# Memory rows loaded behind the weights and kept unsplit, and matmul operands placed at chosen offsets modulo 256 bytes, in a one-core decoder-layer kernel

## The chip, the cores and the metric

The program runs on one core of one Trainium2 chip. The metric is the device time of one execution in microseconds, the median of several runs. A profiled execution gives the rows shown below; its own time stands beside the median. Engines are called by their names in the profile: PE (TensorE matmuls), PEld (TensorE weight loads), DVE (VectorE), ACT (ScalarE), POOL (GpSimd) and SP (SyncE, which here only issues DMAs).

## The reference

One layer of a hybrid decoder for two request groups with shared weights: 256 prompt rows and 8 rows of single-token decoding, together T = 264 rows of width 2048, all in float32.

```python
x = layer_norm(ALPHA * x + 0.5 * swiglu(x, ffn1_w1, ffn1_w3, ffn1_w2), ln1_g, ln1_b)     # FFN 1
mix, sh, cv, wkv = parallel_mixer(x, shift_prev, conv_prev, wkv_prev, p)                # RWKV-7 heads and convolution
x = layer_norm(ALPHA * x + mix, ln2_g, ln2_b)
x = layer_norm(ALPHA * x + mem_attend(x, mk, mv, w_mq, w_mo), ln3_g, ln3_b)             # 4 heads over 256 memory tokens
x = layer_norm(ALPHA * x + 0.5 * swiglu(x, ffn2_w1, ffn2_w3, ffn2_w2), ln4_g, ln4_b)    # FFN 2
mk, mv = mem @ w_mk, mem @ w_mv                                                         # prompt group, 256 memory rows
```

The FFNs are 2048 to 5632 and back. The outputs are the two groups' rows, the new states, and the memory keys and values `mk` and `mv`.

## The kernel before

Activations lie transposed: the 2048 features are 16 tiles of 128 partitions, each with 264 columns. Every float32 operand of a large product is split in two: a rounded high part (`hi`, made by an ACT copy to float32r) and the rest (`lo`, made by a DVE subtraction), at `split_from` (L153 to L155). A product is then three matmuls in `mm3` (L263 to L267): the activations are the moving operand, a 128 x 128 block of the weights is the stationary one, and the order is hi weights with hi activations, hi weights with lo activations, lo weights with hi activations. In `gemm` (L280) every feature tile k of the activations meets two such blocks, so one k is six matmuls in a row, all of them on the same two activation tiles (three where a weight tile is only 128 columns wide).

The weights stream from HBM. `fetch` (L214) issues 512 KB loads on SP into three `raw` tiles, `prepare` (L232) splits each into one of four `whi` and four `wlo` tiles of 128 x 1024, and `chunk` hands them to the matmuls, 24 matmuls for each. The order of the weight tiles is a plan made at the start (`plan_add`); raw loads run up to three tiles ahead of the splits, and the splits up to four ahead of the matmuls.

The stages follow the reference: FFN 1 (the trace's first 790 us), four units of the memory keys and values (`mem_kv`, L1292), the mixer, its output projection, the other units with the attention, its output projection, and FFN 2 (from about 1790 us). Side jobs (`Side`, `start`, `pump`) are Python generators that a planner steps between the matmuls. The framework then orders each engine's instructions; an instruction without a dependency on the matmuls may be issued much earlier than the place where the generator made it. `tc.issue_after(x)` puts the instructions of its block behind `x` where they are on the same engine's queue.

Operands of the large matmuls live here:
- `xh{k}`, `xl{k}`: the 16 split tiles of the layer's input (pool `act`), also the first 16 gate tiles of FFN 2
- `gh{i}`, `gl{i}`: the 22 gate tiles of half an FFN (pools `ffn1` and, for 16 to 21, `ffn2`)
- `rh{k}`, `rl{k}`: 16 split tiles of 266 columns (pool `raw`), the memory rows during the attention and then the rows that FFN 2 starts from; the normalised rows enter FFN 2 through them
- `mh{k}`, `ml{k}`: the split memory rows of 256 columns (pool `mem`)

A pool hands out its tiles one behind the other in the order in which their tags are first asked for, and pads a tile's row to a multiple of 32 bytes. The pools stand behind each other: `const`, `wraw`, `whi`, `wlo`, `act`, `tmp`, and then either `mem` with `ffn1` behind it, or `mix`, or `raw` with `att` or `ffn2` behind it. A row of 264 float32 is 1056 bytes, four times 256 and 32 more.

The memory rows are loaded in `mem_rows` (L1277, started at the 300th step of FFN 1) in four loads of 512 KB on SP (`split_in`, L169), split at once, and both parts are written to HBM by 32 DMAs on POOL (L1284). `mem_reload` (L1286) reads them back by 32 DMAs on POOL (L1290) once the mixer's pool is closed, during the mixer's output projection. Four tables (`lnv`, `mv`, `cw`, `sst`) are loaded by `loaded` (L138, DMA at L141) at the 100th step. `rst`, a constant of the recurrence with 520 columns, is a tile of `const` filled by two POOL memsets (L631, L632).

Of the kernel before, what the change touches and what calls it, by code (L numbers as in the profile page):

```python
# [8 lines left out]
F32 = mybir.dt.float32  # L9
F32R = mybir.dt.float32r  # L10
I32 = mybir.dt.int32
AF = mybir.ActivationFunctionType
ALU = mybir.AluOpType
# [5 lines left out]
KD = 16  # L19
TP = 256  # L20
TB = 8
T = TP + TB
DFF = 5632
# [4 lines left out]
C = 64  # L28
NC = TP // C
NP = 2 * NC  # L30
# [23 lines left out]
class Builder:  # L54
    def __init__(self, tc, I, O, es):
        self.tc, self.nc, self.I, self.O = tc, tc.nc, I, O
        P = lambda name, bufs, **kw: es.enter_context(tc.tile_pool(name=name, bufs=bufs, **kw))
        self.const = P("const", 1)
        self.wraw = P("wraw", NRAW)
        self.whi = P("whi", NSPLIT)  # L60
        self.wlo = P("wlo", NSPLIT)
        self.act = P("act", 1)
        self.tmp = P("tmp", 2)
        self.acc = P("acc", 4, space=PSUM)
        self.mis_stack = es.enter_context(ExitStack())
        self.banks()
        self.dram = P("dram", 1, space=DRAM)
        self.n = 0
        self.t = 0.0
        self.sides = []  # L70
        self.plan, self.raws, self.split = [], [], []
        self.nraw = self.nsplit = self.nused = self.nres = 0

    def banks(self, held=0):

        self.mis_stack.close()
        P = lambda name, bufs: self.mis_stack.enter_context(self.tc.tile_pool(name=name, bufs=bufs, space=PSUM))
        self.mis = P("mis", 4 - held)
        self.held = P("held", held) if held else None

    def uid(self, s):
        self.n += 1
# [55 lines left out]
    def loaded(self, name, shape):  # L138

        t = self.ct(shape, name)  # L140
        self.nc.sync.dma_start(t, self.I[name])  # L141
        return t

    def hold(self):

# [13 lines left out]
        lo = [self.act.tile([128, T], F32R, tag=f"xl{k}", name=self.uid("xl")) for k in range(KD)]  # L159
        return hi, lo  # L160

    def split_in(self, pool, src, n, hi, lo, between=None):

        W = 4

        def load(h):
            t = pool.tile([128, W, T], F32, tag="nat", name=self.uid("nat"), bufs=2)[:, :, :n]
            if between is None or h:
                self.nc.sync.dma_start(t, src[:, W * h : W * h + W])  # L169
            else:  # L170

                self.nc.sync.dma_start(t[:, :1], src[:, :1])
                between(1, (slice(0, 2),))
                self.nc.sync.dma_start(t[:, 1:], src[:, 1:W])
                between(1, (slice(2, 4),))
            return t

        loaded = [load(0)]
        if between is not None:
            between(EARLY)  # L180
        for h in range(KD // W):
            if h + 1 < KD // W:
                loaded.append(load(h + 1))
            yield LOAD
            for k in range(W):
                kk = W * h + k
                with self.hold():
                    self.first.append(self.split_from(loaded[h][:, k], hi[kk], lo[kk]))
                yield 1.5
# [24 lines left out]
    def fetch(self, ahead=NRAW, parts=(slice(None),)):  # L214
        nc = self.nc
        if parts[0].start == 2:
            src, kk, cc = self.plan[0]
            nc.sync.dma_start(
                self.raws[0].rearrange("p (k c) -> p k c", c=cc)[:, parts[0]],
                src.rearrange("(k p) c -> p k c", p=128)[:, parts[0]],  # L220
            )
            return
        while self.nraw < len(self.plan) and self.nraw < self.nsplit + ahead:
            src, kk, cc = self.plan[self.nraw]
            raw = self.wraw.tile([128, 1024], F32, tag="raw", name=self.uid("raw"))[:, : kk * cc]
            dst, src = raw.rearrange("p (k c) -> p k c", c=cc), src.rearrange("(k p) c -> p k c", p=128)
            for k in parts:
                nc.sync.dma_start(dst[:, k], src[:, k])
            self.raws.append(raw)
            self.nraw += 1  # L230

# [338 lines left out]
    def mixer_consts(self):  # L570
        nc, I, tc = self.nc, self.I, self.tc
# [14 lines left out]
        gp = nc.gpsimd  # L586
# [40 lines left out]
            for o in QS:  # L627
                gp.tensor_copy(self.lm[o, l], m[o, o])

        self.rst = self.ct([128, NP, C + 1], "rst")  # L630
        gp.memset(self.rst, 1.0)  # L631
        gp.memset(self.rst[:, :, 0:1], 0.0)  # L632

    def mcol(self, n, j, w=1):
        c = MV[n] + j
# [580 lines left out]
    def mixer(self, pool, P):  # L1216
        nc = self.nc
        self.mx = pool
        H = 30
        self.rows = {}  # L1220
        self.sa, self.vk = self.ct([128, 8, TB], "sa"), self.ct([128, 8, TB], "vk")
        self.last = self.mt("last", (128, 27, TB + 1))
        done = Side(self.tc, iter(()), 0)
        done.done = True
        self.convs, self.heads, self.decs, self.tails, self.cL = [done], [done], [done], {}, []
        self.S = [{} for _ in range(4)]
        for u in MIX_ORDER.split():
            kind, g = u[0], int(u[1])
            if kind == "l":
                yield from self.lora(P[u])  # L1230
            elif kind in "kvr":
                yield from self.rw_part(kind, g, P[u])
            else:
                yield from self.conv_part([2 * g, 2 * g + 1] if kind == "p" else [g], P[u])
# [42 lines left out]
    def mem_rows(self, pool):  # L1277
        self.mh = [pool.tile([128, TP], F32R, tag=f"mh{k}", name=self.uid("mh")) for k in range(KD)]
        self.ml = [pool.tile([128, TP], F32R, tag=f"ml{k}", name=self.uid("ml")) for k in range(KD)]
        yield from self.split_in(pool, self.I["mem"], TP, self.mh, self.ml)  # L1280
        self.mkeep = [self.dram.tile([2, 128, TP], F32R, tag=f"mem{k}", name=self.uid("mem")) for k in range(KD)]
        for k in range(KD):
            for i, t in enumerate((self.mh, self.ml)):
                self.nc.gpsimd.dma_start(self.mkeep[k][i], t[k])  # L1284

    def mem_reload(self):  # L1286
        self.mh, self.ml = self.rawtiles()
        for k in range(KD):
            for i, t in enumerate((self.mh, self.ml)):
                self.nc.gpsimd.dma_start(t[k][:, :TP], self.mkeep[k][i])  # L1290

    def mem_kv(self, unit, dest):  # L1292

# [358 lines left out]

PRETURN = 5
RAW, RENORM = 2, 0.6
TS = 384
LASTCOLS = [(1536, 256), (1792, 128), (1920, 128)]
CONV_GAP = 2.5
# [25 lines left out]
def program(tc, I, O):  # L1683
    with ExitStack() as es:
# [8 lines left out]
        P2 = b.ffn_plan(I["ffn2_w1"][0], I["ffn2_w3"][0], I["ffn2_w2"][0])  # L1693

        with tc.tile_pool(name="mem", bufs=1) as mpool:
            with tc.tile_pool(name="ffn1", bufs=1) as pool:
                b.xs = b.load_x(mpool)

                def ffn1():
# [29 lines left out]
        def after():  # L1729
            mix.close()  # L1730
            b.raw = es.enter_context(tc.tile_pool(name="raw", bufs=1))
            b.att_start(att.enter_context(tc.tile_pool(name="att", bufs=1)))

        b.drive(b.mixer_out(PX, after))
# [8 lines left out]
        att.close()  # L1743
        b.banks()
        with tc.tile_pool(name="ffn2", bufs=1) as pool:

            def ffn2():
                b.L = yield from b.ffn(pool, P2, b.L)
# [80 lines left out]
```

## Time and profile before

| what | us |
|---|---|
| median of 3 runs | 2542.96 (2537.16 to 2549.2) |
| the profiled execution's own time | 2542.35 |
| its span, first to last instruction | 2540.6 |

| engine | busy us | share of the span | instructions |
|---|---|---|---|
| PE | 2483.8 | 98% | 22328 |
| PEld | 2428.6 | 96% | 22328 |
| DVE | 1573.6 | 62% | 2529 |
| ACT | 1190.5 | 47% | 1786 |
| POOL | 282.1 | 11% | 466 |

Matmuls overlap, so one matmul's duration in the trace (some 0.28 us) is not what it costs; the distance from one start to the next is. A window of the trace names how many matmuls touch it, and the window's length over that count gives the distance. The two or so matmuls that straddle a window's edges are counted in it, so that 2.3 (0.28 us over 0.12 us) is taken off a window's count.

### The profile page before, as it was taken

What the parts mean: (1) busy time and instruction counts of PE and PEld (TensorE: products, weight loads), DVE (VectorE), ACT (ScalarE), POOL (GpSimd) and SP (SyncE); (2) the same over time, 40 slices, a digit from 0 to 9 for tenths busy, and PEclk for the clock granted to TensorE, in tenths of its full rate; (3) what the DMA queues carried; (4) which work ended last, traced back from release to release, by engine and by line L of the source; (5) the groups of instructions that cost most, each with busy time, mean ns of one, the idle gap of its engine ahead of it and who ended that gap; (6) DMA issues with size and microseconds to landing.
All of it is one profiled execution on the core that took longest, in us unless ns stands there. A gap on an engine that the chain in (4) does not pass through costs nothing. (4 is left out here: it accounts for less than half of the span.)

```text
span 2540.6 us, 53466 instructions
## 1 busy us (share of the span) xinstructions
PE 2483.8 (98%) x22328; PEld 2428.6 (96%) x22328; DVE 1573.6 (62%) x2529; ACT 1190.5 (47%) x1786; POOL 282.1 (11%) x466
## 2 busy tenths in 40 slices
PE   8999999999999999999989999999999999999998
PEld 8999999999999988988889889999999999999998
DVE  5644444444657598799767567779545445454564
ACT  5444333444445555455636355657444333444443
POOL 2400000000000001000130222220133400000000
PEclk9999999999999999999999999999999999999999
DMA  9655555555557754544386789975677755555553
GB/s 294 201 178 181 179 182 181 181 182 180 171 178 219 225 158 125 154 129 136 128 277 225 260 297 318 330 218 189 196 217 212 222 182 183 181 178 181 175 174 126
DMA packets 460083, 502.09 MB, mean 198 GB/s; under 512 B 22800, under 2 KB 427536, under 8 KB 459840
## 3 DMA queue, kind: packets, MB, share of 16 engines
q1 hardware_dynamic: 417840, 417.09, 52.3%
q0 software_dynamic: 28864, 71.42, 9.0%
q10 hardware_dynamic: 13136, 10.15, 1.2%
q8 instruction: 175, 2.87, 0.5%
q14 instruction: 68, 0.56, 0.1%
HBM read 479.86 MB, written 18.73 MB: 196 GB/s over the span
## 5 line engine op out<-in xcount | busy, mean ns | idle before, releaser
L155 DVE TENSOR_TENSOR wlo<-raw,whi 128x1024 fp32r<-128x1024 f32 (+1 forms) x791 | 959.1, 1213 | 865.7 <-ACT whi L154 861.4
L154 ACT ACTIVATE whi<-raw 128x1024 fp32r<-128x1024 f32 (+1 forms) x791 | 823.0, 1041 | 1052.1 <-PE acc L266 881.0
L265 PE MATMUL acc<-xh,whi 128*128 128x264 f32 x2864 | 832.2, 292 | 20.3 <-DVE y L1208 7.8
L266 PE MATMUL acc<-xl,whi 128*128 128x264 f32 x2864 | 821.9, 287 | 0.6 <-DVE xl L155 0.6
L267 PE MATMUL acc<-xh,wlo 128*128 128x264 f32 x2864 | 819.1, 287 | 1.2 <-issue 0.7
L265 PEld LDWEIGHTS acc<-xh,whi 128*128 128x128 f32 x2864 | 544.0, 190 | 29.6 <-issue 8.4
L266 PEld LDWEIGHTS acc<-xl,whi 128*128 128x128 f32 x2864 | 545.2, 190 | 3.9 <-DVE xl L155 1.0
L267 PEld LDWEIGHTS acc<-xh,wlo 128*128 128x128 f32 x2864 | 543.2, 190 | 3.3 <-DVE wlo L155 1.1
L265 PE MATMUL acc<-rh,whi 128*128 128x264 f32 (+2 forms) x1600 | 458.5, 287 | 0.2 <-ACT lnx L359 0.2
L267 PE MATMUL acc<-rh,wlo 128*128 128x264 f32 (+2 forms) x1600 | 455.9, 285 | 0.0
L266 PE MATMUL acc<-rl,whi 128*128 128x264 f32 (+2 forms) x1600 | 454.9, 284 | 0.0
L265 PE MATMUL acc<-gh,whi 128*128 128x264 f32 x1408 | 400.4, 284 | 1.7 <-ACT lnx L359 1.7
L267 PE MATMUL acc<-gh,wlo 128*128 128x264 f32 x1408 | 400.8, 285 | 0.0
L266 PE MATMUL acc<-gl,whi 128*128 128x264 f32 x1408 | 400.5, 284 | 0.0
L265 PEld LDWEIGHTS acc<-rh,whi 128*128 128x128 f32 x1600 | 302.1, 189 | 2.6 <-ACT lnx L359 0.5
L266 PEld LDWEIGHTS acc<-rl,whi 128*128 128x128 f32 x1600 | 301.2, 188 | 1.2
L267 PEld LDWEIGHTS acc<-rh,wlo 128*128 128x128 f32 x1600 | 301.5, 188 | 0.2
L265 PEld LDWEIGHTS acc<-gh,whi 128*128 128x128 f32 x1408 | 265.3, 188 | 2.0 <-ACT lnx L359 1.9
L267 PEld LDWEIGHTS acc<-gh,wlo 128*128 128x128 f32 x1408 | 264.9, 188 | 0.1
L266 PEld LDWEIGHTS acc<-gl,whi 128*128 128x128 f32 x1408 | 264.6, 188 | 0.0
L1141 DVE SCALAR_TENSOR_TENSOR y<-u,cw,y 128x256 f32<-128x256 f32 x240 | 111.7, 479 | 0.6
L1121 POOL MEMSET u<- 128x30 f32 x8 | 1.0, 131 | 787.9 <-DMA out<-mo 745.0
(350 smaller groups left out, 2132.0 us busy)
## 6 DMA issues: line engine op xcount, KB each, us to landing
raw<-in_ffn_w SPq DMA_DIRECT2D x509, 512.0 KB, 3.6
raw<-in_w_in SPq DMA_DIRECT2D x86, 512.0 KB, 3.6
raw<-in_w_mk SPq DMA_DIRECT2D x32, 512.0 KB, 3.3
raw<-in_w_mv SPq DMA_DIRECT2D x32, 512.0 KB, 5.4
raw<-in_w_out SPq DMA_DIRECT2D x32, 512.0 KB, 4.0
kv<-in_cache_mem_k POOLq DMA_DIRECT2D x32, 512.0 KB, 6.7
raw<-in_w_mq SPq DMA_DIRECT2D x32, 512.0 KB, 6.1
kv<-in_cache_mem_v POOLq DMA_DIRECT2D x32, 512.0 KB, 6.0
```

Source lines behind the costliest of these rows:

```text
L154: a = self.nc.scalar.activation(hi, src, AF.Copy)
L155: return a, self.nc.vector.tensor_tensor(lo, src, hi.bitcast(F32), ALU.subtract)
L265: nc.tensor.matmul(out, wh, xh, start=start, stop=False)
L266: nc.tensor.matmul(out, wh, xl, start=False, stop=False)
L267: self.mark = nc.tensor.matmul(out, wl, xh, start=False, stop=stop)
L1121: nc.gpsimd.memset(u[:, 0:H], 0.0)
L1141: V.scalar_tensor_tensor(c[:, :TP], u[:, i : i + TP], w(i), c[:, :TP], ALU.mult, ALU.add)
```

## The change

Four things change.

1. **Places.** Unused gap tiles and an order of first use fix where the moving operands begin modulo 256 bytes. `places` lays out pool `act`: a gap of 224 bytes, then for each two feature tiles `xh`, `xl`, `xh`, `xl`, followed by four `y` tiles or a gap of 128 bytes. `gate_places` does the like for the gate tiles with the gaps `GAPS[1]` and `GAPS[3]`; `rh` and `rl` stand in pairs with a gap of 128 bytes between pairs behind a first gap of `GAPS[2]`; pool `mem` begins with a gap of `GAPS[0]`.
2. **Held loads.** `behind` puts the loads of the four tables and of the memory rows behind the weight load that SP issued last where the generator made them.
3. **The kept memory rows.** The raw rows are written to HBM by four DMAs of 512 KB on POOL, straight from the loaded tiles. The reload is 16 DMAs of 128 KB on POOL into the `rl` tiles, and each is split again by an ACT copy and a DVE subtraction in place.
4. **`rst`** moves from pool `const` into pool `mix`, and its two memsets to the mixer's start.

```diff
     def __init__(self, tc, I, O, es):
...
         self.act = P("act", 1)
+        self.places()
         self.tmp = P("tmp", 2)
...
+    def place(self, pool, *tags):
+
+        for t in tags:
+            if isinstance(t, int):
+                if t:
+                    pool.tile([128, t // 4], F32, tag=self.uid("gap"), name=self.uid("gap"))
+            else:
+                tag, cols, dt = t
+                pool.tile([128, cols], dt, tag=tag, name=self.uid(tag))
+
+    def places(self):
+
+
+        order = [224]
+        for q in range(KD // 2):
+            for k in (2 * q, 2 * q + 1):
+                order += [(f"xh{k}", T, F32R), (f"xl{k}", T, F32R)]
+            order += [(f"y{m}", T, F32) for m in range(4 * q, 4 * q + 4)] if q < KD // 4 else [128]
+        self.place(self.act, *order)
+
+    def gate_places(self, pool, first, gap):
+        order = [gap]
+        for i in range(first, DFF // 256, 2):
+            for k in (i, i + 1):
+                order += [(f"gh{k}", T, F32R), (f"gl{k}", T, F32R)]
+            order.append(128)
+        self.place(pool, *order)
...
     def loaded(self, name, shape):
 
         t = self.ct(shape, name)
-        self.nc.sync.dma_start(t, self.I[name])
+        with self.behind():
+            self.nc.sync.dma_start(t, self.I[name])
         return t
+
+    def behind(self):
+
+        return self.tc.issue_after(self.lastraw.ins)
...
-    def split_in(self, pool, src, n, hi, lo, between=None):
+    def split_in(self, pool, src, n, hi, lo, between=None, keep=None):
...
-            if between is None or h:
+            if keep is not None:
+                with self.behind():
+                    self.nc.sync.dma_start(t, src[:, W * h : W * h + W])
+                self.nc.gpsimd.dma_start(keep[:, W * h : W * h + W], t)
+            elif h:
                 self.nc.sync.dma_start(t, src[:, W * h : W * h + W])
...
-                nc.sync.dma_start(dst[:, k], src[:, k])
+                self.lastraw = nc.sync.dma_start(dst[:, k], src[:, k])
...
-        self.rst = self.ct([128, NP, C + 1], "rst")
-        gp.memset(self.rst, 1.0)
-        gp.memset(self.rst[:, :, 0:1], 0.0)
...
         self.last = self.mt("last", (128, 27, TB + 1))
+        self.rst = self.mt("rst", (128, NP, C + 1))
+        nc.gpsimd.memset(self.rst, 1.0)
+        nc.gpsimd.memset(self.rst[:, :, 0:1], 0.0)
...
-        yield from self.split_in(pool, self.I["mem"], TP, self.mh, self.ml)
-        self.mkeep = [self.dram.tile([2, 128, TP], F32R, tag=f"mem{k}", name=self.uid("mem")) for k in range(KD)]
-        for k in range(KD):
-            for i, t in enumerate((self.mh, self.ml)):
-                self.nc.gpsimd.dma_start(self.mkeep[k][i], t[k])
+        self.mkeep = self.dram.tile([128, KD, TP], F32, tag="mem", name=self.uid("mem"))
+        yield from self.split_in(pool, self.I["mem"], TP, self.mh, self.ml, keep=self.mkeep)
 
     def mem_reload(self):
+
         self.mh, self.ml = self.rawtiles()
         for k in range(KD):
-            for i, t in enumerate((self.mh, self.ml)):
-                self.nc.gpsimd.dma_start(t[k][:, :TP], self.mkeep[k][i])
+            hi, lo = self.mh[k][:, :TP], self.ml[k][:, :TP]
+            raw = lo.bitcast(F32)
+            self.nc.gpsimd.dma_start(raw, self.mkeep[:, k])
+            self.nc.scalar.activation(hi, raw, AF.Copy)
+            self.nc.vector.tensor_tensor(lo, raw, hi.bitcast(F32), ALU.subtract)
...
+GAPS = 128, 224, 96, 128
...
         with tc.tile_pool(name="mem", bufs=1) as mpool:
+            b.place(mpool, GAPS[0])
             with tc.tile_pool(name="ffn1", bufs=1) as pool:
+                b.gate_places(pool, 0, GAPS[1])
...
             b.raw = es.enter_context(tc.tile_pool(name="raw", bufs=1))
+            for k in range(KD):
+                b.place(b.raw, 128 if k else GAPS[2], (f"rh{k}", T + 2, F32R), (f"rl{k}", T + 2, F32R))
...
         with tc.tile_pool(name="ffn2", bufs=1) as pool:
+            b.gate_places(pool, KD, GAPS[3])
```

## Rows read from the trace of the kernel before

**Rows 1.** The page's busy times by engine, and the costliest matmul groups of its section 5 (line, engine, operation, tiles, shapes, count | busy, mean ns | idle before).

```profile
PE 2483.8 (98%) x22328; PEld 2428.6 (96%) x22328; DVE 1573.6 (62%) x2529; ACT 1190.5 (47%) x1786; POOL 282.1 (11%) x466
...
L265 PE MATMUL acc<-xh,whi 128*128 128x264 f32 x2864 | 832.2, 292 | 20.3 <-DVE y L1208 7.8
...
L265 PE MATMUL acc<-rh,whi 128*128 128x264 f32 (+2 forms) x1600 | 458.5, 287 | 0.2 <-ACT lnx L359 0.2
...
L265 PE MATMUL acc<-gh,whi 128*128 128x264 f32 x1408 | 400.4, 284 | 1.7 <-ACT lnx L359 1.7
```

**Rows 2.** Windows by stage: the stretch in us, its length, busy time and count of PE, PEld, DVE, ACT, POOL, the granted clock, the DMA share, GB/s. FFN 1 first products; FFN 2 first products; FFN 1 second products; FFN 2 second products; then most of the memory's first key unit, and its first value unit (256 columns each; in the value unit the weights move and the memory rows are stationary).

```profile
420.00:670.00 250.00, 250.00 (x2056) 250.00 (x2055) 121.06 (x130) 105.07 (x131) 0.00 (x0) 1.00 0.57 180
2140.00:2400.00 260.00, 260.00 (x2133) 260.00 (x2132) 128.11 (x137) 108.66 (x137) 2.42 (x5) 1.00 0.58 180
290.00:400.00 110.00, 110.00 (x907) 110.00 (x906) 51.13 (x56) 40.44 (x41) 0.00 (x0) 1.00 0.57 181
2010.00:2120.00 110.00, 110.00 (x902) 110.00 (x902) 54.09 (x57) 41.03 (x43) 13.04 (x12) 1.00 0.57 189
792.80:812.60 19.80, 19.80 (x170) 19.80 (x169) 19.52 (x44) 15.46 (x26) 0.00 (x0) 1.00 0.68 216
812.80:835.60 22.80, 22.80 (x192) 22.80 (x191) 14.77 (x21) 17.16 (x32) 0.00 (x0) 1.00 0.87 262
```

**Rows 3.** The order of time on PE in FFN 2's second products (start us, duration, line, operation, tiles): the first of the six matmuls of gate tiles 0, 1, 3, 7 and 8, and then of tiles 17 and 19.

```profile
2488.12 0.28 PE L265 MATMUL acc<-gh,whi 128*128 128x264 f32 x1
...
2488.84 0.28 PE L265 MATMUL acc<-gh,whi 128*128 128x264 f32 x1
...
2490.29 0.29 PE L265 MATMUL acc<-gh,whi 128*128 128x264 f32 x1
...
2493.27 0.29 PE L265 MATMUL acc<-gh,whi 128*128 128x264 f32 x1
...
2494.00 0.28 PE L265 MATMUL acc<-gh,whi 128*128 128x264 f32 x1
...
2500.61 0.28 PE L265 MATMUL acc<-gh,whi 128*128 128x264 f32 x1
...
2502.06 0.29 PE L265 MATMUL acc<-gh,whi 128*128 128x264 f32 x1
```

**Rows 4.** The same view in FFN 1's second products: the first of the six matmuls of two gate tiles, with one tile between them.

```profile
357.98 0.28 PE L265 MATMUL acc<-gh,whi 128*128 128x264 f32 x1
...
359.44 0.28 PE L265 MATMUL acc<-gh,whi 128*128 128x264 f32 x1
```

**Rows 5.** SP's queue in order of time near the start (start us, time over the merged issues, line, operation, tiles), and below it the DMA view of 20 to 70 us (its mean rate, and issues by tile with KB each and us to landing).

```profile
27.46 0.50 SPq L141 DMA_DIRECT2D lnv<-in_lnv  x1
...
34.01 0.43 SPq L169 DMA_DIRECT2D nat<-in_mem  x1
...
47.28 1.03 SPq L169 DMA_DIRECT2D nat<-in_mem  x1
```

```profile
DMA packets 15721, 15.48 MB, mean 310 GB/s; under 512 B 1036, under 2 KB 15588, under 8 KB 15716
...
nat<-in_mem SPq DMA_DIRECT2D x4, 512.0 KB
mem<-mh POOLq DMA_DIRECT2D x16, 128.0 KB, 5.7
```

**Rows 6.** PE in order of time around its longest waits near the start, and around the two in the mixer's output projection (start us, duration, line, operation, tiles [idle before and what ended it]).

```profile
60.34 0.59 PE L265 MATMUL acc<-xh,whi 128*128 128x264 f32 x1 [3.56 <-ACT lnx L359]
...
62.08 0.59 PE L265 MATMUL acc<-xh,whi 128*128 128x264 f32 x1 [0.71 <-ACT lnx L359]
62.46 0.42 PE L266 MATMUL acc<-xl,whi 128*128 128x264 f32 x1
62.68 0.42 PE L267 MATMUL acc<-xh,wlo 128*128 128x264 f32 x1
```

```profile
1283.29 0.56 PE L265 MATMUL acc<-xh,whi 128*128 128x264 f32 x1 [4.71 <-DVE y L1208]
```

```profile
1308.60 0.56 PE L265 MATMUL acc<-xh,whi 128*128 128x264 f32 x1 [2.43 <-DVE y L1208]
```

**Rows 7.** Windows as in Rows 2: a stretch of lowered clock near the start, the stretch in which the memory rows are read back, and one of lowered clock within it.

```profile
59.30:66.10 6.80, 5.05 (x21) 4.75 (x22) 4.84 (x7) 4.00 (x7) 4.54 (x9) 0.50 1.21 323
1270.00:1300.00 30.00, 25.29 (x190) 25.11 (x189) 16.82 (x29) 8.36 (x9) 21.07 (x39) 0.89 1.10 317
1281.20:1288.10 6.90, 4.81 (x22) 4.84 (x23) 4.41 (x8) 1.55 (x3) 4.63 (x9) 0.51 1.19 346
```

**Rows 8.** Waits between 1262 and 1290 us (who waited for whom: us in total, times, longest).

```profile
ACT whi L154 <- DMA raw<-in_w_out: 7.8, 2, 6.8
```

**Rows 9.** The instructions of single tiles (line, engine, operation, tiles, count: shortest, median and longest ns, first and last start us): the memory rows' splits, half of their reload, and the first memset of `rst` with its readers.

```profile
L154 ACT ACTIVATE mh<-nat x16: 396/402/420, 40.6 to 58.7; 128x256 fp32r<-128x256 f32 x16
L155 DVE TENSOR_TENSOR ml<-nat,mh x16: 417/420/426, 41.1 to 59.2; 128x256 fp32r<-128x256 f32 x16
```

```profile
L1290 POOL DMA_DIRECT2D rh<-mem x16: 528/536/598, 1269.5 to 1294.0; - x16
```

```profile
L731 DVE TENSOR_TENSOR_SCAN L<-rst,sig x4: 1233/1234/1241, 894.3 to 1175.9; 128x520 f32<-128x520 f32 x4
L631 POOL MEMSET rst<- x1: 536/536/536, 1.5 to 1.5; 128x520 f32 x1
```

More of the change, by code (lines that the diff above doesn't have):

```diff
@@ L56, in __init__ @@
         self.tc, self.nc, self.I, self.O = tc, tc.nc, I, O
+        self.n = 0
         P = lambda name, bufs, **kw: es.enter_context(tc.tile_pool(name=name, bufs=bufs, **kw))
@@ L67, in __init__ @@
         self.dram = P("dram", 1, space=DRAM)
-        self.n = 0
         self.t = 0.0
```

## The prediction

> **What bounds the kernel now.** The page comes first: PE is busy for 98% of the span, DVE for 62%, ACT for 47% [rows 1]. PE sets the end, and only two things can move it: the distance between matmuls that stand in a row, and the waits. The windows by stage give the distance. In FFN 1 it is 250 / (2056 - 2.3) = 121.7 ns in the first products and 121.6 in the second; in FFN 2 it is 122.0 and 122.3 [rows 2]. The clock granted is 1.00 in all four, the upper level, 2.4 GHz, at which 264 columns are 110 ns. So some 12 ns of each matmul are not columns. Of the whole, 3 x (2864 + 1600 + 1408) = 17616 matmuls are of this kind [rows 1], 2.15 ms of the 2.54. The order of time on PE then says whether the 12 ns are the same for all: they aren't. In FFN 2's second products the six matmuls of a tile take from 0.72 us upward, and the stretch of tiles 3 to 6 is slower than that of tiles 0 to 2 [rows 3]. Last come the waits: some 4 us near the start, 7 us in the mixer's output projection, each followed by a stretch at the lower clock [rows 6, 7].
>
> **Which addresses these tiles have.** The weights' three pools hold tiles of 4096 bytes, so all stationary blocks share one offset modulo 256; call it zero. Pool `act` follows at zero, and each 1056-byte tile moves the next by 32. So `xh{k}` and `xl{k}` both stand at 32k modulo 256 (sixteen tiles apart is 512), and FFN 2's gate tiles 0 to 7 at 0, 32, 64, ..., 224. Behind `act` (48 tiles, nothing modulo 256) and `tmp` (13 tiles of 1056, 160 modulo 256) pool `mem` begins at 160, and so does everything in it and the gate tiles of FFN 1: `gh0` 160, `gl0` 192, `gh1` 224, `gl1` 0, and on. In FFN 2, tiles 16 to 21 go the same way.
>
> After the change the sum is: `act` begins with 224, that is -32, so `xh` of an even k stands at -32, its `xl` at 0, of an odd k at +32 and +64, and the `y` tiles or the gap of 128 bring the next pair back to -32. `act` and `tmp` end at 128, the gap in `mem` makes it 0 for the memory rows, 224 more is -32 for the gate tiles; `rh` stands at -32, `rl` at +32. `rst` moves everything alike, weights too. So the change keeps every large moving operand within -32 to +64, a set that holds half of today's places.
>
> **What the set costs today.** Tiles 0 to 2 (offsets 0, 32, 64) take 2490.29 - 2488.12 = 2.17 us for 18 matmuls, tile 7 (-32) takes 0.73 for 6: 2.90 / 24 = 120.8 ns. Tiles 3 to 6 (96 to 192) take 2493.27 - 2490.29 = 2.98: 124.2 ns [rows 3]. There hi and lo share an offset. Where they alternate as they will, -32 and 0 and then +32 and +64, tiles 17 and 18 of FFN 2 take 1.45 us for 12, 120.8 ns [rows 3], and the same two offsets in FFN 1 take 1.46, 121.7 ns, no better than their stage [rows 4]. Three rows, 120.8, 120.8 and 121.7; the distance also hangs on what came before, and after the change no tile of the slow half comes before. I take 120.8. The ends are the fastest single tile, 0.72 / 6 = 120.0 [rows 3], and the slow half, 124.2.
>
> FFN 2 has 3 x 1600 + 3 x 704 = 6912 of these matmuls at 122.1, all others are 10704, taken at FFN 1's 121.7 though the mixer's and the attention's have no clean window. At 120.8: 6912 x 1.3 + 10704 x 0.9 = 9.0 + 9.6 = **18.6 us** less. At 120.0: 14.5 + 18.2 = 32.7 less. At 124.2: 14.5 + 26.8 = 41.3 more. The 256-column products of the memory are a few hundred; at zero offset they have no row, and the two units, both 160 apart, cost 118.1 and 120.2 [rows 2]: under 2 us either way, left out.
>
> The Trainium skill, in "SBUF — State Buffer" (section "SBUF: two separate sides"), says that of the engine ports "PE, ACT, and DVE's dedicated pair never wait on anyone", and in "TensorE: Matmul & The Clock Gate" (section "Wait — 56ns, not 53.3ns?") that start to start is the columns over 2.4 GHz and some 2.5 ns. By these pages places are worth nothing, and 264 columns would take an estimated 112.5 ns; the rows show 121.7, and 120.8 against 124.2 by tile. I go by the rows and keep that outcome as a rival.
>
> **Held loads.** In the trace the tables and the memory rows are loaded at 27 to 47 us, long before their step of the program, and 2 MB of memory rows come in and 4 MB of their parts go out while 310 GB/s move [rows 5]. There PE waits 3.56 and 0.71 us for split weights [rows 6], and the low clock (0.50, 1.2 GHz) that follows spaces 21 matmuls at 0.22 us, not 0.12 [rows 6, 7]: 2.1 us. Together 6.4 us. After the change the tables go out behind the weight load of step 100, chunk 25, some 73 us in (a chunk is 24 x 0.1217 = 2.9 us), the memory rows behind that of step 300, 219 us in, where the DMA share is about 0.57 and 180 GB/s move, as in FFN 1's windows [rows 2]. Moved with them: 4 + 4 issues on SP of some 0.5 us each, and on POOL 4 writes of 512 KB for 32 of 128 KB. What is late next: the third and fourth memory load wait on SP for a tile that must first be written out and split, and weight loads queue behind; cover is three raw and four split tiles, 20 us. The 16 splits, 0.40 us on ACT and 0.42 on DVE [rows 9], fall where both are half idle. I take **-6.4 us**; ends 0 (the burst makes the same wait later) and -9.
>
> **The reload.** At 1270 to 1300 us the DMA share is 1.10, PE is busy 25.3 of 30 us [rows 7], and ACT's split of a `w_out` tile waits 6.8 us for its load [rows 8]; behind it PE waits 4.71 and later 2.43 us and loses some 22 x 0.10 us at the low clock [rows 6, 7]: 9.3 us. The reload is 4 MB of the 9.5 that move there; 2 MB less is 6.6 us at 317 GB/s. Sixteen POOL issues of 0.54 us go [rows 9]. Against it, ACT and DVE get 16 x 0.40 = 6.4 and 16 x 0.42 = 6.7 us of splits, with 21.6 and 13.2 us idle in the stretch; but each waits for a DMA, and weight splits queue behind it in order. I take **-3 us**; ends -9.3 (both waits gone) and +9.3 (as much again).
>
> **`rst`.** Its memset, 0.54 us on POOL, goes from 1.5 us to the mixer's start, at about 840; the first reader is at 894 [rows 9] and POOL is nearly idle. Nothing.
>
> Sum: 18.6 + 6.4 + 3 = 28 us. The profiled execution took 2542.35 us with 1.75 outside its span, 0.6 under the median of 2542.96: 2542.35 - 28 = **2514 us**.
>
> **The rivals.**
> - *The set runs at its best.* With no slow tile ahead the matmuls settle at 120.0: 2542.35 - 32.7 - 9.4 = 2500. For: the distance depends on the tiles before, and 0.72 us exists. Against: +64 and -32 took more.
> - *Places are worth nothing.* By the skill's rule, or because FFN 1's alternating tiles at 121.7 are what remains: 2542.35 - 9.4 = 2533.
> - *The reload's splits block ACT.* The waits there double: 2542.35 - 18.6 - 6.4 + 9.3 = 2527.
> - *A fixed pattern locks in a slow phase*, the one on the slower side. Today the offsets wander through all eight and a slow stretch ends by itself after four tiles; twelve matmuls that repeat unchanged through the whole kernel can stay slow. At 124.2: 2542.35 + 41.3 - 9.4 = 2574. It decides from a mean of 122.4, where the loss eats the 9.4. For it: a value unit at a constant offset holds 120.2 for its whole length where a key unit has 118.1 [rows 2]. Against: the slow stretch lies at the offsets that the change leaves.
>
> **How the numbers follow.** Forecast 2514 us with 0.49; the set at its best 0.20; places worth nothing 0.18; blocked ACT 0.05; slow lock 0.08. About 0.5%, 12.7 us, is what a measurement of this kernel can tell from no change: so 2533 is within it, 2527, 2514 and 2500 are faster, 2574 slower. Faster 0.74, same 0.18, slower 0.08. The range takes in all but the slow lock and the far end of the best case: 2500 - 12 for waits that all go, and 2533 + 5 for a burst that waits later: 2488 to 2538.
>
> **What would show it.** Places: FFN 1's window of 250 us holds about 2072 matmuls in place of 2056, FFN 2's of 260 about 2154 in place of 2133, and the tiles' six-matmul times no longer range from 0.72 to 0.75. Held loads: no load of memory rows before 200 us, no PE wait of 3.6 us and no low clock at 59 us, and none at 220. Reload: 16 issues in the stretch, and the wait of the `w_out` split under 6.8 us. Wrong would be unchanged windows, or a wait of ACT on the reloaded tiles that is followed by a wait of PE.

## The result, and the profile after

The changed kernel takes 2523.69 us (median of 5 runs, 2520.73 to 2528.88) against 2542.96: a ratio of 0.9928, with a 95% interval of 0.9902 to 0.9953. That is 19.3 us by the medians, where 28 were forecast; beside the experiments below it came out at 0.9931 (0.9913 to 0.9950). The profiled execution took 2526.33 us, 16.0 less than the profiled one of before. The page of the kernel after, its span and busy times, which answer to [rows 1]:

```profile
span 2524.6 us, 53420 instructions
...
PE 2470.9 (98%) x22328; PEld 2417.2 (96%) x22328; DVE 1582.8 (63%) x2545; ACT 1195.0 (47%) x1802; POOL 261.7 (10%) x422
```

PE still sets the end, with the same 22328 matmuls. DVE and ACT have 16 instructions more (the second split), POOL 44 fewer: 16 reloads for 32, 4 writes for 32. Windows of the kernel after, with the columns of [rows 2]: the low-clock stretch of before near the start, the two stretches in which the memory rows now come in, the two FFN 1 stages, the reload, the two FFN 2 stages:

```profile
59.30:66.10 6.80, 6.80 (x59) 6.80 (x58) 3.83 (x7) 2.91 (x3) 6.17 (x14) 1.00 0.55 173
215.00:245.00 30.00, 30.00 (x250) 30.00 (x249) 18.15 (x26) 15.54 (x26) 1.77 (x2) 1.00 0.77 254
245.00:275.00 30.00, 30.00 (x250) 30.00 (x249) 16.72 (x24) 14.21 (x23) 1.51 (x2) 1.00 0.76 239
...
290.00:400.00 110.00, 110.00 (x909) 110.00 (x907) 51.17 (x55) 41.10 (x42) 0.00 (x0) 1.00 0.60 182
420.00:670.00 250.00, 250.00 (x2060) 249.92 (x2058) 121.60 (x130) 104.53 (x128) 0.00 (x0) 1.00 0.59 180
...
1265.00:1295.00 30.00, 22.68 (x173) 22.50 (x172) 18.74 (x39) 14.43 (x25) 9.13 (x16) 0.89 0.90 313
...
2010.00:2120.00 110.00, 110.00 (x908) 110.00 (x908) 53.48 (x58) 41.02 (x42) 5.11 (x8) 1.00 0.59 188
2140.00:2400.00 260.00, 260.00 (x2140) 259.89 (x2140) 130.06 (x141) 110.66 (x138) 1.94 (x4) 1.00 0.59 180
```

Read as before (length over count less 2.3), FFN 1 has 250 / 2057.7 = 121.5 ns where it had 121.7, its second products 121.3 (121.6), FFN 2 121.6 and 121.5 (122.0 and 122.3). The forecast wanted 2072 matmuls in FFN 1's window and 2154 in FFN 2's; there are 2060 and 2140. So the places gave, but far less than 120.8 ns would. At the start the wait and the low clock of [rows 6, 7] are gone (59 matmuls in the same 6.8 us, not 21), and none appears where the memory rows now come in.

The order of time on PE in the kernel after, in FFN 2's second products: the first of the six matmuls of one gate tile, and of the tile 29 further on.

```profile
2470.87 0.28 PE L303 MATMUL acc<-gh,whi 128*128 128x264 f32 x1
...
2491.99 0.29 PE L303 MATMUL acc<-gh,whi 128*128 128x264 f32 x1
```

(2491.99 - 2470.87) / 29 = 0.728 us for each tile, and every tile between has 0.72 or 0.73. The range of [rows 3], 0.72 to 0.75, is gone as forecast; but the level at which it settled is 121.4 ns, not 120.8. SP's queue in order of time, the loads that were held:

```profile
82.14 0.50 SPq L171 DMA_DIRECT2D lnv<-in_lnv  x1
...
227.85 1.05 SPq L204 DMA_DIRECT2D nat<-in_mem  x2
...
262.76 0.50 SPq L204 DMA_DIRECT2D nat<-in_mem  x1
```

The tables come at 82 us and the memory rows from 228 us on (forecast: 73 and 219), not at 27 and 34 [rows 5]. In the reload, PE, DVE and ACT in order of time, and the waits of 1255 to 1300 us of the kernel after:

```profile
1277.38 0.56 PE L303 MATMUL acc<-xh,whi 128*128 128x264 f32 x1 [7.32 <-DVE y L1243]
```

```profile
1275.67 1.23 DVE L189 TENSOR_TENSOR wlo<-raw,whi 128x1024 fp32r<-128x1024 f32 x1 [3.07 <-ACT whi L188]
1276.82 1.44 DVE L1243 TENSOR_TENSOR y<-y,acc 128x264 f32<-128x264 f32 x4
```

```profile
1266.44 0.42 ACT L1328 ACTIVATE rh<-rl 128x256 fp32r<-128x256 f32 x1 [4.18 <-DMA y<-keep]
...
1273.92 0.78 ACT L1328 ACTIVATE rh<-rl 128x256 fp32r<-128x256 f32 x2 [1.31 <-DMA rl<-mem]
1274.60 1.04 ACT L188 ACTIVATE whi<-raw 128x1024 fp32r<-128x1024 f32 x1
```

```profile
PEld acc L303 <- ACT rh L1328: 7.5, 1, 7.5
PE acc L303 <- DVE y L1243: 7.3, 1, 7.3
ACT whi L188 <- DMA raw<-in_w_out: 4.7, 2, 3.2
```

ACT's longest wait for a `w_out` tile fell from 6.8 to 3.2 us, and the second PE wait (2.43) with its low clock is gone. But the first grew from 4.71 to 7.32 us. The row names DVE, which empties an accumulator; but DVE itself had just waited 3.07 us for ACT's split of a `w_out` tile, and the weight load of the same matmul waited for ACT. The splits of the reloaded tiles stand in ACT's queue and wait there for POOL's DMAs, 4.18 us for the first and 1.31 us for a later one. By the record of landings the `w_out` tile was there at 1272.4 us, and ACT split it at 1274.6, behind the wait of 1.31 us. So 2.2 of the 7.32 us are blocking by ACT; up to 1272.4 us the tile's load was still under way.

One difference was not in the sum of the forecast. It lies behind the last operation of POOL. The last row of the chain of waits (start, us), first of the kernel before, whose span is 2540.6, then of the kernel after, whose span is 2524.6:

```profile
2531.18 1.22 POOLq L1825
```

```profile
2518.84 1.22 POOLq L1870
```

From there to the end of the span it is 2540.6 - 2532.4 = 8.2 us before and 2524.6 - 2520.1 = 4.5 us after, with the same work ahead of it. The records show what it is: a closing DRAIN on POOL that ends 7.44 us after POOL's last operation before, and 3.36 us after. SP, which waits for the last output to land, is done 4.5 us ahead of the end before and 0.8 us after, there 0.4 us behind the DRAIN. So the DRAIN set the end before and SP sets it now, and of the 4.08 us by which the DRAIN is shorter 3.7 reach the end.

### The profile page after: what moved, and what is told of

It reads as the page before. It is cut to its first block, busy times and chain, and to the rows that moved or that the text cites. A ratio compares the mean times of both kernels' runs of the same rounds, so it can differ in the third digit from the quotient of the medians.

```text
span 2524.6 us, 53420 instructions
## 1 busy us (share of the span) xinstructions
PE 2470.9 (98%) x22328; PEld 2417.2 (96%) x22328; DVE 1582.8 (63%) x2545; ACT 1195.0 (47%) x1802; POOL 261.7 (10%) x422
## 3 DMA queue, kind: packets, MB, share of 16 engines
q0 software_dynamic: 20992, 67.22, 8.4%
## 5 line engine op out<-in xcount | busy, mean ns | idle before, releaser
L397 ACT ACTIVATE lnx<-acc 128x264 f32<-128x264 f32 x84 | 32.4, 386 | 64.8 <-PE acc L305 64.8
```

The costliest lines, as they stand in the source:

```text
L397: self.lastfn = self.nc.scalar.activation(*args, **kw)
```

## The experiments

To size a part in a trace, the distances between successive large products' matmuls are averaged over all that are under 160 ns (some 17,100 of 17,400 in each trace), which leaves the waits out. Before: 121.86 ns. After: 121.43.

**1. Each part alone, or left out.** Four kernels, run beside the kernel before (2541.2 us there, 22 runs). `rst` is moved in all of them.

```diff
# no_places: the changed kernel without any gap
-        self.places()
...
-            b.place(mpool, GAPS[0])
...
-                b.gate_places(pool, 0, GAPS[1])
...
-                b.place(b.raw, 128 if k else GAPS[2], (f"rh{k}", ...), (f"rl{k}", ...))
...
-            b.gate_places(pool, KD, GAPS[3])
# held_only: no_places, and the memory rows split at once and kept in two parts
# kept_only: no_places, and without "with self.behind():" around the loads
# places_only: the gaps, without behind(), and kept in two parts
```

> The changed kernel without its gaps and its order of first use; the loads stay held, the memory rows are kept unsplit, rst stays moved. Theory A, read from the two traces: the places shortened the start-to-start distances by 7.4 us in all and the rest of the gain is the start. Then this kernel takes 7 to 9 us more than the changed one, 2531 to 2534 us with a before of 2543, its distance in FFN 1 is 121.7 ns again and in FFN 2 122.0 to 122.3, and there is still no wait of PE near 60 us. Theory B, the terms of the forecast: places are worth 18.6 us, so 2542 us, level with the kernel before. Theory C: places are worth nothing in time, 2524 us.

> The kernel before with the gaps and the order of first use alone (and rst moved); the loads are not held, the memory rows are kept split as before. Theory A: 7 to 9 us less than before, 2534 to 2536 us, with the distances of the changed kernel, 121.4 ns in FFN 1 and 121.1 to 121.6 in FFN 2, and the 3.6 us wait of PE near 57 us still there. Theory B: 18.6 us less, 2524 us. Theory C: 2543 us.

> The kernel before with the held loads alone (and rst moved): the tables and the memory rows are loaded behind the weights, the rows are split and both parts written by 32 DMAs, no gaps. Theory A: the whole 7.7 us at the start comes from this part: 2535 us, no wait of PE over 1 us near 57 us and no lowered clock before 900 us. Rival: half the gain at the start came from the halved write-out (2 MB for 4 MB); then the 32 writes make PE wait where they now fall, at 220 us and later, and the time is 2539 us or more.

> The kernel before with the memory rows kept unsplit and split again at the reload alone (and rst moved): no held loads, no gaps. Theory A: within 3 us of before, 2540 to 2546 us: the reload's gain at 1270 us (the two waits of 4.7 and 2.4 us become one) is given back by 7 us more waits in the attention. Theory B, the forecast: 3 us less there, and a little at the start, where 2 MB less are written: 2538 to 2540 us. Rival: the splits at the reload block ACT and PE, 2547 us or more.

| kernel | median us | ratio to before (95%) | mean distance, ns |
|---|---|---|---|
| no_places | 2528.89 | 0.9955 (0.9941 to 0.9969) | 121.87 |
| places_only | 2533.14 | 0.9975 (0.9962 to 0.9987) | 121.48 |
| held_only | 2534.53 | 0.9969 (0.9957 to 0.9981) | 121.87 |
| kept_only | 2535.83 | 0.9977 (0.9967 to 0.9987) | 121.87 |

The places are worth 0.0025 x 2541 = 6.4 us alone, and (0.9955 - 0.9928) x 2541 = 7 us on top of the rest; by distance it is 0.38 to 0.44 ns x 17616 = 6.7 to 7.8 us. Theory A's 7.4 holds, the forecast's 18.6 falls, and so does "worth nothing". The three kernels without places repeat the distance of before to 0.01 ns. Windows of places_only, then of no_places:

```profile
420.00:670.00 250.00, 250.00 (x2062) 250.00 (x2061) 121.56 (x130) 104.99 (x131) 0.00 (x0) 1.00 0.59 180
...
2140.00:2400.00 260.00, 260.00 (x2140) 259.89 (x2140) 129.43 (x141) 110.41 (x138) 1.93 (x4) 1.00 0.58 180
```

```profile
420.00:670.00 250.00, 250.00 (x2056) 250.00 (x2056) 121.15 (x129) 104.68 (x130) 0.00 (x0) 1.00 0.59 180
...
2140.00:2400.00 260.00, 260.00 (x2132) 260.00 (x2131) 129.06 (x140) 109.42 (x136) 1.93 (x4) 1.00 0.58 179
```

2062 and 2140 against 2056 and 2132: the counts go with the gaps and with nothing else.

The held loads are worth 0.0031 x 2541 = 7.9 us. PE around its waits near the start in places_only, whose loads are not held, and the window of held_only there:

```profile
58.62 0.59 PE L300 MATMUL acc<-xh,whi 128*128 128x264 f32 x1 [4.25 <-ACT lnx L394]
...
60.30 0.59 PE L300 MATMUL acc<-xh,whi 128*128 128x264 f32 x1 [0.65 <-ACT lnx L394]
```

```profile
59.30:66.10 6.80, 6.80 (x58) 6.80 (x57) 3.99 (x7) 2.94 (x3) 6.16 (x14) 1.00 0.59 168
```

held_only still writes 4 MB in 32 DMAs, so the gain is that of the moved loads, not of the halved write. Over all fourteen traces, the 201st matmul with low weights starts at 88.3 to 90.2 us in the three kernels with early loads and at 80.9 to 83.4 in the eleven with held ones: means of 89.0 and 82.1, 6.9 us.

Keeping the rows unsplit is worth 0.0023 x 2541 = 5.8 us, more than either theory gave it (experiment 4). The rival, splits that block ACT and PE to 2547 us or more, falls by its price; that ACT blocks at all is seen above. Alone, the three parts make 6.4 + 7.9 + 5.8 = 20.1 us of the change's 19.3.

**2. Other places.** If the place relative to the weights counts, moving all moving operands by 128 bytes must put them into the slow half; if only the repeated pattern or the step from tile to tile counts, a shift of all does nothing. Three further kernels, with one run each, shift the families by other amounts; only their windows are read.

```diff
# all_128 (shift_32, shift_64 and shift_96 change the same numbers)
-        order = [224]
+        order = [96]
...
-GAPS = 128, 224, 96, 128
+GAPS = 0, 96, 96, 128
```

> The changed kernel with every large moving operand (xh, xl, gate tiles, rh, rl) 128 bytes further modulo 256, the weights where they were: all now stand at 96 to 192, the half that was slow by tile in the kernel before. Nothing else differs. Theory A, the place relative to the weights sets the distance: by the kernel before's tiles at 96 to 192 (753, 742, 732, 749 ns for six) 124 ns in FFN 1 and FFN 2 in place of 121.4 and 121.6, 2.5 x 17616 = 44 us more than the changed kernel, 2568 us. Theory B, what counts is that the places repeat in a fixed pattern, not where they are: 121.4 to 121.6 ns, 2524 us. Theory C, the weights do not enter and only the step from one moving tile to the next does: the same as B in every window to 0.1 ns.

> A look for the windows by stage: x tiles of FFN 1 and the first sixteen gate tiles of FFN 2 32 bytes further (0, 32 and 64, 96), gate tiles of FFN 1 32 bytes back (-64, -32 and 0, 32), rh and rl 32 further (0 and 64). Theory A, weighted by the tiles of the kernel before: x 122.0 ns, FFN 1 gates 121.9, rh and rl 120.3. Theory B or C: 121.4, 121.4, 121.1 to 121.6 as in the changed kernel.

> A look: x tiles 64 further (32, 64 and 96, 128), FFN 1 gate tiles 64 back (160, 192 and 224, 0), rh and rl 64 further (32 and 96). Theory A by the tiles of before: x 123.2 ns, gates 121.8, rh and rl 122.8. Theory B or C: as in the changed kernel, 121.4, 121.4, 121.1 to 121.6.

> A look: x tiles 96 further (64, 96 and 128, 160), FFN 1 gate tiles 160 further (128, 160 and 192, 224), rh and rl 32 back (192 and 0). Theory A by the tiles of before: x 122.9 ns, gates 123.3, rh and rl 123.2. Theory B or C: as in the changed kernel, 121.4, 121.4, 121.1 to 121.6.

all_128 took 2539.04 us (12 runs), 0.9996 of before (0.9982 to 1.0010): the whole gain of the change, and not only that of its places, was lost. Its mean distance is 122.35 ns: (122.35 - 121.43) x 17616 = 16 us more than the changed kernel, and the medians differ by 15. The following are its windows (FFN 1 second and first products, FFN 2 second and first), and then those of shift_32, shift_64 and shift_96:

```profile
290.00:400.00 110.00, 110.00 (x899) 110.00 (x897) 50.24 (x55) 40.55 (x41) 0.00 (x0) 1.00 0.59 178
420.00:670.00 250.00, 250.00 (x2039) 250.00 (x2038) 120.17 (x130) 103.55 (x128) 0.00 (x0) 1.00 0.57 178
2010.00:2120.00 110.00, 110.00 (x898) 110.00 (x898) 55.00 (x60) 41.68 (x46) 14.21 (x14) 1.00 0.58 187
2140.00:2400.00 260.00, 260.00 (x2136) 260.00 (x2135) 130.60 (x142) 110.07 (x138) 3.86 (x8) 1.00 0.58 180
```

```profile
290.00:400.00 110.00, 110.00 (x899) 110.00 (x898) 50.91 (x55) 40.87 (x41) 0.00 (x0) 1.00 0.59 179
420.00:670.00 250.00, 250.00 (x2064) 250.00 (x2063) 122.51 (x132) 103.98 (x128) 0.00 (x0) 1.00 0.58 181
...
2140.00:2400.00 260.00, 260.00 (x2142) 259.88 (x2142) 133.38 (x155) 111.04 (x140) 1.94 (x4) 1.00 0.58 180
```

```profile
290.00:400.00 110.00, 110.00 (x906) 110.00 (x905) 50.69 (x56) 40.91 (x41) 0.00 (x0) 1.00 0.60 181
420.00:670.00 250.00, 250.00 (x2048) 250.00 (x2047) 120.55 (x128) 103.74 (x129) 0.00 (x0) 1.00 0.58 180
...
2140.00:2400.00 260.00, 260.00 (x2128) 260.00 (x2128) 127.74 (x137) 109.69 (x137) 1.93 (x4) 1.00 0.58 179
```

```profile
290.00:400.00 110.00, 110.00 (x899) 110.00 (x898) 51.11 (x55) 40.88 (x41) 0.00 (x0) 1.00 0.59 179
420.00:670.00 250.00, 250.00 (x2056) 250.00 (x2056) 121.45 (x131) 103.90 (x127) 0.00 (x0) 1.00 0.58 179
...
2140.00:2400.00 260.00, 260.00 (x2130) 260.00 (x2129) 128.61 (x139) 109.55 (x137) 1.93 (x4) 1.00 0.58 180
```

| operands | shift in bytes | measured ns | expected from single tiles |
|---|---|---|---|
| x, FFN 1 | 0 / 32 / 64 / 96 / 128 | 121.5 / 121.3 / 122.2 / 121.7 / 122.7 | - / 122.0 / 123.2 / 122.9 / 124 |
| gates, FFN 1 | 0 / -32 / -64 / 160 / 128 | 121.3 / 122.7 / 121.7 / 122.7 / 122.7 | - / 121.9 / 121.8 / 123.3 / 124 |
| rh and rl, FFN 2 | 0 / 32 / 64 / -32 / 128 | 121.6 / 121.5 / 122.3 / 122.2 / 121.9 | - / 120.3 / 122.8 / 123.2 / 124 |

Theories B and C fall: the same pattern at another distance from the weights takes another time. An absolute address falls too. Moving `rst` shifts the weights and the operands together by 2080 bytes, 32 modulo 256, which is the step from one `x` tile to the next. Yet, matmul by matmul, the distances in FFN 1's window of no_places follow those of the kernel before with a correlation of 0.96, and of 0.02 when they are set one tile apart. Theory A holds in kind only. All 15 measured values lie between 121.3 and 122.7 ns, while the single tiles promised 120.3 to 124; for the gates, -32 is as slow as 160. A tile's six-matmul time, read out of a mixed sequence, doesn't add up to that of a fixed one. Nor is it shown that 256 bytes is the right modulus. In FFN 1's first products of the kernel before, equal places modulo 256 come back after 8 tiles, but the distances there have a correlation of 0.03 at 48 matmuls (8 tiles) and of 0.94 at 96 (16 tiles). Whether the modulus is larger or something else with a longer cycle counts is open.

**3. The best of the shifts**, all families 32 bytes further, beside the changed kernel once more.

```diff
-        order = [224]
+        order = [0]
...
-GAPS = 128, 224, 96, 128
+GAPS = 96, 0, 96, 128
```

> The changed kernel with all large moving operands 32 bytes further modulo 256 (x and gate tiles at 0, 32 and 64, 96; rh and rl at 0 and 64), the best of the shifts looked at. If the windows of the look hold: FFN 1 121.2 ns in place of 121.4, its second products 121.1 to 121.4, FFN 2 121.1 and 121.4 in place of 121.4 and 121.6; some 0.2 to 0.3 ns x 17616 = 4 to 5 us less than the changed kernel, 2519 us. Rival: the 5 us that the look was faster were spread of the attention stage; then level with the changed kernel, 2523 us.

> The changed kernel once more, for a second trace and beside the next three: 2520 to 2529 us. The windows of FFN 1 and FFN 2 and the time from POOL's last operation to the end of the span should repeat to 0.1 ns and 0.1 us; what doesn't repeat is the spread of one kernel. If the attention stage (1457 to about 1690 us, 232 us in the first trace) comes out at 225 us this time, its 7 us over the kernel before are spread and no cost of the change.

best_32: 2517.74 us (6 runs), ratio 0.9907 (0.9888 to 0.9925); the changed kernel beside it 2523.26, ratio 0.9931 (0.9913 to 0.9950). The intervals overlap, so the times alone don't separate the two; the distances do: 121.16 ns against 121.43 and, in the second trace, 121.49, so 0.27 to 0.33 x 17616 = 5 to 6 us, and the medians differ by 5.5. Windows of best_32:

```profile
290.00:400.00 110.00, 110.00 (x911) 110.00 (x910) 52.07 (x56) 40.93 (x41) 0.00 (x0) 1.00 0.61 183
420.00:670.00 250.00, 250.00 (x2064) 249.88 (x2063) 122.76 (x135) 105.03 (x131) 0.00 (x0) 1.00 0.58 180
2010.00:2120.00 110.00, 110.00 (x910) 110.00 (x909) 52.56 (x58) 41.97 (x43) 2.33 (x5) 1.00 0.59 185
2140.00:2400.00 260.00, 260.00 (x2143) 259.88 (x2142) 133.85 (x158) 110.24 (x138) 1.93 (x4) 1.00 0.58 180
```

So with this pattern the change's own shift was a good one, and 32 bytes more is a little better.

**4. The end, and the reload in the changed kernel.** keep_48 issues the same bytes of the write-out in 48 DMAs in place of 4, so that POOL has as many DMAs as before; split_kept undoes the unsplit keeping alone.

```diff
# keep_48
-                self.nc.gpsimd.dma_start(keep[:, W * h : W * h + W], t)
+                for k in range(W):
+                    for c0, c1 in ((0, 64), (64, 128), (128, n)):
+                        self.nc.gpsimd.dma_start(keep[:, W * h + k, c0:c1], t[:, k, c0:c1])
# split_kept
-                self.nc.gpsimd.dma_start(keep[:, W * h : W * h + W], t)
...
+        for k in range(KD):
+            for i, t in enumerate((self.mh, self.ml)):
+                self.nc.gpsimd.dma_start(self.mkeep[k][i], t[k])
...
-            self.nc.gpsimd.dma_start(raw, self.mkeep[:, k])
-            self.nc.scalar.activation(hi, raw, AF.Copy)
-            self.nc.vector.tensor_tensor(lo, raw, hi.bitcast(F32), ALU.subtract)
+            for i, t in enumerate((self.mh, self.ml)):
+                self.nc.gpsimd.dma_start(t[k][:, :TP], self.mkeep[k][i])
```

> The changed kernel with the write-out of the unsplit memory rows cut into 48 DMAs on POOL in place of 4, the same bytes, so that POOL issues 316 DMAs in all as in the kernel before and not 272. Theory A: the time between POOL's last operation and the end of the span goes by the number of DMAs that POOL has issued: 8.2 us as in the kernel before in place of 4.5, so the end comes 3.7 us later, 2527 us. Theory B: it goes by packets or by the reload, not by the count: 4.5 us stay (or 6 at most), and the time is 2523 to 2525 us.

> The changed kernel with the memory rows split at once, both parts written by 32 DMAs and read back by 32, loads held and places as changed. Theory A, from the traces so far: the reload's stage (1285 to 1375 us) is 4.2 us longer, the end 3.7 us longer, and if the unsplit reload also makes the attention stage longer (mean 229.8 us in seven traces with it, 224.6 in three without), that stage is 5 us shorter: 3 us slower in all, 2527 us. Theory B: the attention's difference is spread: 8 us slower, 2531 us. The difference of the two pairs without the other parts (held_only against no_places, before against kept_only) was 5.7 and 5.4 us.

keep_48: 2526.82 us (0.9935, 0.9912 to 0.9958), 3.6 us over the changed kernel beside it; the two intervals overlap, and it is the trace that decides. Its page's span and POOL count, and the last row of its chain:

```profile
span 2529.9 us, 53485 instructions
...
PE 2475.2 (98%) x22328; PEld 2421.8 (96%) x22328; DVE 1578.6 (62%) x2545; ACT 1196.1 (47%) x1802; POOL 285.1 (11%) x466
```

```profile
2519.97 1.22 POOLq L1872
```

2529.9 - 2521.2 = 8.7 us from POOL's last operation to the end, and the DRAIN ends 7.93 us after it: theory A. The packets of POOL's queue don't explain it: 21952 here, 20992 in the changed kernel, 28864 in the kernel before. The write-out is issued between 230 and 275 us and is paid for some 2250 us later. In all fourteen traces the DRAIN takes 7.44 us (the four kernels with 316 DMAs in the old split), 7.93 (keep_48) or 3.35 to 3.36 (the nine with 272), whatever else differs: 4.08 / 44 = 93 ns for each, on average.

split_kept: 2529.18 us (0.9945, 0.9924 to 0.9966), 5.9 us over the changed kernel (the intervals overlap), between the two theories. The attention, from the first to the last start of its products `po` (count, shortest, median and longest ns, first and last start), in the kernel before, in split_kept, and in the changed kernel:

```profile
L1532 PE MATMUL po<-vh,eye x32: 387/397/401, 1503.1 to 1684.1; 128*8 128x512 f32 x32
```

```profile
L1570 PE MATMUL po<-vh,eye x32: 387/394/405, 1485.1 to 1668.3; 128*8 128x512 f32 x32
```

```profile
L1571 PE MATMUL po<-vh,eye x32: 387/392/412, 1493.2 to 1679.8; 128*8 128x512 f32 x32
```

181.0 and 183.2 us against 186.6 (the expectations counted the stage between two fixed matmuls, some 40 us wider). In the four traces with split rows it is 181.0 to 183.8 (mean 182.3), in the ten with unsplit rows 184.3 to 188.8 (mean 186.8), with no overlap. So in the profiled executions unsplit keeping costs the attention 4.5 us, though PE and SP have the same instructions in the same order there. The stretch of the reload (2801st to 3201st matmul with low weights) gains 1.7 us by the means of these two groups (218.2 to 216.5) and 1.6 to 3.5 us in the pairs that differ in the keeping alone, and the end gains 3.7.

These three make 0.9 us, and the timed pairs say 5.4 (before and kept_only), 5.6 (held_only and no_places) and 5.9. Without the attention's loss they would make 5.4. In the seven timed sets with unsplit rows (the changed kernel stands in two) the profiled execution is above its set's median by 0.5 to 7.2 us (mean 4.0); in the four with split rows it is above or below (mean -1). So the loss in the attention may belong to profiled executions alone. That is argued, not shown, since other executions leave no trace. What makes the attention slower stays open as well.

## Why the prediction came out as it did

The direction and the range held, 2523.7 in 2488 to 2538. The sum was 28 us and the result is 19. Part of that closeness is luck: the largest term was more than twice too big, and 3.7 us that the forecast didn't have made up for some of it. The terms, one by one:

- **Places, 18.6 forecast, 7 measured.** The mechanism was right: the distance hangs on the places of the moving tiles relative to the weights, as all_128 and no_places show, and the tiles' times became equal. The failing step is "I take 120.8". Three rows stood there, two from FFN 2's gate tiles and one from FFN 1 with the alternating offsets at 121.7, "no better than their stage"; I went with the two. The third was the one with the sequence that the change would make, and the measured 121.3 to 121.6 lies by it. The reason given for the choice, that after the change no slow tile comes before, did not hold: with the sequence fixed, the fast tiles became slower too. A small miscount adds to it: 576 of the 17616 matmuls, 192 of each 1600, are products of 256 columns for the memory rows and not FFN 2's, 0.7 us of the 18.6.
- **Places worth nothing** would have been 2533 and was refuted by places_only and no_places. The Trainium skill's rule, in "TensorE: Matmul & The Clock Gate" (section "Wait — 56ns, not 53.3ns?"), gives 264 / 2.4 + 2.5 = 112.5 ns, an estimate from that page. No FFN window here shows that. They have 121.1 to 122.8 ns, with the place of the operands as the only difference between all_128 and the changed kernel.
- **The slow lock** at 124.2 ns did not come, neither in the changed kernel nor where it was sought: a fixed pattern in the slow half took 122.35. **The set at its best**, 120.0, did not come either: the lowest mean of any kernel here is 121.16.
- **Held loads, 6.4 forecast, 6.9 to 7.9 measured.** Right, with its place, its waits and the clock; what was late next (the wait for a tile to be split) cost nothing, as PE's full windows at 59, 215 and 245 us show.
- **Reload, 3 forecast, 1.7 measured in its stretch (1.6 to 3.5 in pairs).** The size is about right, the way there is not. ACT's wait for the `w_out` tile fell, but one of the prediction's own signs of being wrong came: ACT waits on the reloaded tiles, and a wait of PE follows. The first PE wait grew by 2.6 us, with 2.2 us of blocking by ACT in it, while the second, of 2.43, went. The rival's price for that, 9.3 us, did not come.
- **The end, nothing forecast, 3.7 measured.** The write-out was costed by its bytes and by its issues on POOL; that DMAs which POOL issued long ago lengthen its closing DRAIN stands in no row ahead of POOL's last operation. The prediction read the chain only as far as PE.
- **`rst`, nothing forecast.** No trace shows a cost; its memsets are at 832 us, ahead of the first reader at 885.

## What to carry to other kernels

A rate that is read from single items of a mixed sequence must not be put on a uniform sequence: take the row whose sequence is like the new one, or run the sequence itself once. Where start-to-start distances are above the columns' time, shift the moving operands against the stationary ones in steps of 32 bytes and read one window for each; here the best and the worst of the shifts run for the whole kernel were some 21 us apart. A wait that a row puts down to one engine may start on another: follow it a step further, to what that engine waited for. Count what is issued on POOL as well as its bytes, and read the trace to the very end of the span.

## What the runs showed of the hardware

- The distance between two matmuls of 264 columns, at 2.4 GHz and with no wait, is 121.1 to 122.8 ns by stage in the FFNs, and moves with the place of the moving operand relative to the stationary one (tried in steps of 32 bytes). Moving weights and operands together (`rst` out of `const`, 2080 bytes) changed nothing: 121.86 and 121.87 ns, and the same distances matmul by matmul. That places repeat every 256 bytes is not shown.
- Kernels with the same places repeat that mean to 0.07 ns from trace to trace (121.43 to 121.50 in five), those without gaps to 0.01, so a few tenths of a ns can be read from one trace where whole-kernel times spread by 10 us.
- POOL's closing DRAIN grew from 3.36 to 7.44 us with 44 more DMAs issued on POOL, 93 ns each on average, though they are issued 2250 us earlier (keep_48). It is not in proportion to the whole count (316 and 272), so not every DMA can cost that; which of them do wasn't tried.
